# Hybrid decoder layer: fourth query projection ahead of the third x projection, and one y projection beside the last value products

## The chip, the cores and the metric

The kernel runs on one core of a Trainium2 chip. The core has five engines with instruction queues of their own: TensorE (PE; its weight loads are listed as PEld), VectorE (DVE), ScalarE (ACT), GpSimd (POOL) and SyncE (SP, which here only issues DMAs). Each queue runs in the order in which it was written. The metric is the device time of one execution in microseconds (us); the median of several runs counts.

## The reference

One layer works on 16 meta tokens and 1024 tokens of width 1024. What bears on this case:

```python
u = rmsnorm(h, g_pre_mix[l])
z = u @ w_in[l]
q, k, v, xr, yr = jnp.split(z, split_at, axis=-1)     # 512, 128, 128, 512, 512 columns
attn = sliding_window_attention_with_sinks(q, k, v, attn_sinks[l])   # window 128, 8 heads
xr = causal_depthwise_conv(xr, conv_w[l], conv_b[l])  # 4 taps
hr = rg_lru(xr, w_a[l], b_a[l], w_x[l], b_x[l], lru_lambda[l])
rec = (jax.nn.gelu(yr.astype(jnp.float32)) * hr).astype(h.dtype)
mix = jnp.concatenate([attn.astype(h.dtype), rec], axis=-1) @ w_out[l]
h = h + rmsnorm(mix, g_post_mix[l])
...
f = jnp.square(jax.nn.relu(u @ w_ff1[l])) @ w_ff2[l]
h = h + rmsnorm(f, g_post_ffn[l])
```

The recurrence `rg_lru` computes two sigmoid gates from `xr`, a decay from one of them, and a scan along the tokens.

## The kernel before

Everything is float32. For each product an operand is split into a high part (a cast on ACT, L95) and a low part (a subtraction on DVE, L98), and three matmuls (L124 to L126) stand for one.

**The input projection** is cut into chunks of 128 columns. Queries, x and y have four chunks each. A chunk is 48 matmuls of width 512 for queries and y (two pieces, `REAL2`), and 96 matmuls of width 272 or 256 for x (four pieces, `ALL`). The pieces go to the two PSUM banks of the tag "acc". Keys, values, query chunk 0 and x chunk 0 are computed first. A finished piece is evicted: a query piece by two scaled casts on ACT (L116) and two subtractions on DVE (L117), an x piece by a copy on ACT (L394), a y piece by a copy on DVE (L640). Behind each x chunk follows its convolution, four DVE passes (`conv`, L608 and L613).

**Attention** runs over four head pairs j and two halves of the tokens. `scores(j, half, q)` makes the query-key products (L525, L529), the maximum, the exponential on ACT (through `lut`, L82) and a folding of the two window blocks on POOL (L559). `attend(j, half, pairs)` transposes the result (L571), splits it, masks it on POOL (L575) and makes the value products (L585), which are evicted by L598 and L599. It is called one step late, behind the next step's scores.

**Fills.** The remaining projections are put between the steps of attention. `fills` (L648 to L655) is their list: q1, x1, q2, x2, x3, q3 and then y0 to y3. Each call of `next_fill` (L658) issues the load, cast and low part of the following entry's weights and then the matmuls, evictions and convolution of its own entry. Eight calls stand in the attention loop, under `deferred(FILL_LAG)`; the two last, y2 and y3, stand behind the gates (L753).

**What sets the order.** A planner lays out each engine's queue before the run: of the instructions whose inputs and buffers are ready in its own model of time, the one with the lowest order number goes first. The number counts up as the program is written; inside `deferred` it is 1000 higher. So a fill is used where attention has nothing ready. On the chip the order is fixed, and an engine that waits for one instruction does not go on to the next. Buffers have tags, with a fixed count for each tag, and the buffers of a tag go round in the order of the program. Those that matter here are the tag "raw" (2, weights as loaded), "ws" (4, split weights), "d" (4: results of the convolutions 0 to 2, the raw x chunk of 1 to 3, and y0, y2, y3), and "b" (17: among others keys, values, the query pairs, attention's results, convolution 3 and y1).

**Behind attention** come the gates (`gates`, four times: split of the convolved chunk, matmuls, sigmoids), the decays (`decay`), the scan (`recur`), the product with the y chunks (`rec_out`, which ends in a split into `at[half][2]` and `at[half][3]`), the output weights (`load_wo`, `split_wo`) and the output projection `out_mm`. Its first half (kc 0 to 3, `at[half][0]` and `[1]`) needs attention alone; its second half needs the recurrent result. `lut` puts all table functions of ACT into one chain in the order of the program. The feed-forward part, two thirds of the time, follows.

```python
    for j in range(NPAIR):
        for half in range(2):
            if j % 2 == 0 and half == 0:
                at_pair(j // 2)
            sn = scores(j, half, qs[j])
            if True:
                with deferred(FILL_LAG):
                    next_fill()
            if prev is not None:
                attend(*prev)
            prev = (j, half, sn)
    attend(*prev)
```

Of the kernel before, what the change touches and what calls it, by code (L numbers as in the profile page):

```python
# [29 lines left out]
FILL_LAG = 1000  # L30
# [7 lines left out]
def hybrid_layer(  # L38
# [7 lines left out]
    x, out = x[0], out[0]  # L46
# [11 lines left out]
    def slot(tag, shape, dt=F32):  # L58
        uid[0] += 1
        return slab.tile(shape, dt, tag=tag, name=f"{tag}{uid[0]}", bufs=bufs[tag])  # L60

    def pair(tag, shape):
        return slot(tag, shape, F32R), slot(tag, shape, F32R)

    def bank(tag, shape=(P, 512)):
        uid[0] += 1
        return ps.tile(list(shape), F32, tag=tag, name=f"ps_{tag}{uid[0]}")

    def f32(ap):
        return ap.bitcast(F32)  # L70

    @contextmanager
    def deferred(n):
        tc.cur_priority += n
        yield
        tc.cur_priority -= n
# [16 lines left out]
    def split(hi, lo, src, eng=None):  # L93
        if eng is None:
            nc.scalar.copy(hi, src)  # L95
        else:
            eng.tensor_copy(hi, src)
        low = nc.vector.tensor_tensor(lo, src, f32(hi), op=ALU.subtract).ins  # L98
        mark[0] = low.name
        return low  # L100
# [90 lines left out]
    def w_q(j):  # L191
        return load_cols([((w_in, Q_COL + P * j), P)])

    def w_x_chunk(c):
        return load_cols([((w_in, X_COL + P * c), P)])
# [307 lines left out]
    def at_pair(cp):  # L503
        for half in range(2):
            at[half][cp] = pair("b", [P, 2, 512])
# [58 lines left out]
    def attend(j, half, pairs):  # L564
        g = j // 2
        o_ = slot("e", [P, 512])
        for bp, sn in enumerate(pairs):
            mh, ml = pair("c", [P, 4, 2, P])
            pt = bank("pt", (P, 4, P))
            for k in range(4):  # L570
                nc.tensor.transpose(pt[:, k, :], sn[:, k, 0:P], ident)  # L571
            split(mh[:, :, 1, :], ml[:, :, 1, :], pt)
            for m in (mh, ml):
                for side, op, sign in ((0, ALU.is_gt, 1), (1, ALU.is_ge, -1)):
                    nc.gpsimd.affine_select(  # L575
                        out=m[:, :, side, :], in_=f32(m)[:, :, 1, :],
                        pattern=[[0, 4], [-sign, P]], compare_op=op, fill=0.0,
                        base=0, channel_multiplier=sign,
                    )
            po = bank("o", (P, 2, 256))  # L580
            mhv, mlv = (m.rearrange("p (h i) s q -> p h (i s q)", h=2) for m in (mh, ml))

            def av(v, oc, n, pc, first, last):
                for k, m in enumerate((mhv, mlv)):
                    nc.tensor.matmul(  # L585
                        po[:, :, oc : oc + n], v, m[:, :, pc : pc + n],
                        start=first and k == 0, stop=last and k == 1,
                        skip_group_check=True,
                    )

            b = 4 * half + 2 * bp
            av(vk[g][:, b, :], 0, 256, P, True, False)
            av(vm[:, g, :] if b == 0 else vk[g][:, b - 1, :], 0, P, 0, False, False)
            av(vk[g][:, b + 1, :], P, P, 3 * P, False, True)
            c = slice(256 * bp, 256 * bp + 256)
            for h in range(2):
                r, o = HALF[h], HALF[1 - h]
                nc.scalar.copy(o_[r, c], po[o, h, :])  # L598
                nc.vector.tensor_tensor(o_[r, c], po[r, h, :], o_[r, c], op=ALU.add)  # L599
        ah, al = at[half][j // 2]  # L600
        split(ah[:, j % 2, :], al[:, j % 2, :], o_)
# [19 lines left out]
    def fill_q(j):  # L621
        def run(w):
            q, sink = new_q()
            project(w, REAL2, sink)
            qs[j] = q
        return run

    def fill_x(c):
        def run(w):
            xr, sink = new_x()  # L630
            project(w, ALL, sink)
            conv(c, xr, "b" if c == 3 else "d")
        return run
# [12 lines left out]
    qs = [q0] + [None] * 3  # L646
    conv(0, xr0)
    fills = []  # L648
    for kind, j in (("q", 1), ("x", 1), ("q", 2), ("x", 2), ("x", 3), ("q", 3)):
        if kind == "q":  # L650
            fills.append((lambda j=j: w_q(j), fill_q(j)))
        else:
            fills.append((lambda j=j: w_x_chunk(j), fill_x(j)))
# [4 lines left out]
    def next_fill():  # L658
        i = len(loaded) - 1
        if i + 1 < len(fills):  # L660
            loaded.append(fills[i + 1][0]())
        else:
            loaded.append(None)
        fills[i][1](loaded[i])

    prev = None
# [8 lines that stand above are left out]
            if prev is not None:  # L675
                attend(*prev)
            prev = (j, half, sn)
    attend(*prev)


# [14 lines left out]
    def gates(c):  # L695
        ch, cl = pair("b", [P, TT])
        split(ch, cl, xc[c])
        rg[c] = []
        for i in range(2):
            t_ = slot("c", [P, TT])  # L700
            for t0, n in ((0, 348), (348, 348), (696, 344)):
                flip[0] += 1
                acc = bank(("s", "pt", "o")[flip[0] % 3])
                mm3(
                    acc[:, :n], (gh[:, i, c, :], gl[:, i, c, :]),
                    (ch[:, t0 : t0 + n], cl[:, t0 : t0 + n]), True, True,
                )
                lut(
                    t_[:, t0 : t0 + n], acc[:, :n], AF.Sigmoid,
                    bias=prm[:, c, 5 + i : 6 + i],  # L710
                )
            rg[c].append(t_)
        nc.vector.tensor_tensor(t_, t_, xc[c], op=ALU.mult)
# [36 lines left out]

    for c in range(NLRU):
        gates(c)
    for _ in range(2):  # L753
        next_fill()
    for cs in ((0, 1), (2, 3)):
        for c in cs:
            decay(c)
# [597 lines left out]
```

## Time and profile before

| what | before |
|---|---|
| median of 3 runs | 976.04 us (975.72 to 976.45) |
| profiled execution, its own time | 983.92 us |
| profiled execution, its span | 982.2 us |
| PE busy | 951.9 us, 97% of the span |
| DVE, ACT, POOL busy | 662.9, 500.5, 140.3 us |
| attention with its fills | about 62 to 218 us of the span |
| gates to the recurrent result | 218 to 282 us |
| output projection, first matmul | 244.7 us |

Durations are read from one profiled execution, the time of the kernel from the median of the runs. Positions are microseconds from the start of the span. A line such as `L585` is a line of the kernel; where a helper such as `split` or `mm3` writes the instruction, it is the helper's line, and the tile names tell which use it is. Buffer numbers are left out of the names, so that "d" stands for any buffer with the tag "d", and "ps_acc" for a bank with the tag "acc". An idle time in brackets is how long the engine stood still ahead of that instruction, and behind it stands what ended the wait.

### The profile page before, as it was taken

The page shows a single profiled execution, that of the slowest core. Times are in us where ns is not written, and L with a number is a line of the kernel's source. Part 1 is how long each engine was busy: PE and PEld are TensorE (multiplying, and loading weights), DVE is VectorE, ACT ScalarE, POOL GpSimd, SP SyncE. Part 2 cuts the span into 40 slices and gives each one's busy share as a digit, 9 for nine tenths or more (in the row PEclk, how much of TensorE's full clock was granted, in tenths as well). Part 3 has the DMA queues.
Part 4 walks back from the last instruction along what each step waited for, and adds up shares of the span by engine and source line. Part 5 has one row for each costly group of instructions (what it writes and reads, how often), then busy time and mean ns, then how long its engine had stood idle before and what let it go on. Part 6 is the DMA issues. An engine that isn't in the chain of part 4 may idle for free.

```text
span 982.2 us, 12324 instructions
## 1 busy us (share of the span) xinstructions
PE 951.9 (97%) x4654; PEld 797.1 (81%) x4654; DVE 662.9 (67%) x942; ACT 500.5 (51%) x816; POOL 140.3 (14%) x184
## 2 busy tenths in 40 slices
PE   6999989999899999999999999999999999999996
PEld 6998988888788887887788888888888788888885
DVE  5569976755876687656554455468567666779885
ACT  6556562548935554343455556555433343445432
POOL 4016753230002100000000000000011000003011
PEclk9999989999999999999999999999999999999999
DMA  8111001112234465575532264423678766656653
GB/s 282 49 46 42 22 23 44 33 43 65 86 107 150 150 215 192 172 243 192 187 129 86 85 200 121 129 86 108 164 180 194 166 222 207 177 168 150 168 175 85
DMA packets 84794, 131.30 MB, mean 134 GB/s; under 512 B 5464, under 2 KB 48616, under 8 KB 84736
## 3 DMA queue, kind: packets, MB, share of 16 engines
q1 hardware_dynamic: 76912, 109.55, 34.7%
q0 software_dynamic: 7248, 19.40, 9.7%
q10 hardware_dynamic: 576, 1.57, 0.4%
q8 instruction: 36, 0.59, 0.3%
q14 instruction: 22, 0.18, 0.1%
HBM read 110.46 MB, written 18.87 MB: 132 GB/s over the span
## 4 chain that ended last, share of the span: by engine, by line
PE 80%; DVE 7%; ACT 5%; DMA 3%; issue 3%; POOL 2%; DVEq 0%; SPq 0%; ACTq 0%; POOLq 0%
PE ps_acc L124 8%; PE ps_acc L125 8%; PE ps_acc L126 8%; PE ps_pt L125 6%; PE ps_pt L126 6%; PE ps_pt L124 6%; PE ps_s L126 6%; PE ps_s L125 6%; PE ps_s L124 6%; PE ps_o L125 5%; PE ps_o L124 5%; PE ps_o L126 5%; DMA d<-in_w_ff_dram 2%; ACT c L82 1%; DVE ws L98 1%
## 5 line engine op out<-in xcount | busy, mean ns | idle before, releaser
L95 ACT CAST ws<-raw 128x1024 fp32r<-128x1024 f32 (+1 forms) x70 | 71.7, 1024 | 128.1 <-PE ps_o L125 47.5
L98 DVE TENSOR_TENSOR ws<-raw,ws 128x1024 fp32r<-128x1024 f32 (+1 forms) x71 | 85.0, 1197 | 46.4 <-ACT ws L95 46.3
L124 PE MATMUL ps_acc<-a,ws 128*128 128x256 f32 (+2 forms) x256 | 87.6, 342 | 1.4 <-ACT d L394 1.3
L125 PE MATMUL ps_acc<-a,ws 128*128 128x256 f32 (+2 forms) x256 | 86.9, 339 | 0.0
L126 PE MATMUL ps_acc<-a,ws 128*128 128x256 f32 (+2 forms) x256 | 86.2, 337 | 0.0
L98 DVE TENSOR_TENSOR b<-b,b 128x1024 fp32r<-128x1024 f32 (+2 forms) x48 | 57.6, 1200 | 26.3 <-PE ps_o L125 20.1
L95 ACT CAST ws<-e 128x1024 fp32r<-128x1024 f32 x42 | 43.9, 1045 | 59.2 <-PE ps_o L125 35.0
L95 ACT CAST b<-b 128x1024 fp32r<-128x1024 f32 (+2 forms) x48 | 49.5, 1030 | 39.0 <-DVE b L861 38.1
L98 DVE TENSOR_TENSOR ws<-e,ws 128x1024 fp32r<-128x1024 f32 x42 | 51.3, 1222 | 16.1 <-ACT ws L95 16.1
L124 PEld LDWEIGHTS ps_acc<-a,ws 128*128 128x128 f32 x256 | 50.1, 196 | 6.1 <-ACT d L394 1.7
L169 POOL TENSOR_TENSOR rs<-ms,half_pow 128x1 f32<-128x1 f32 (+1 forms) x31 | 22.8, 739 | 221.3 <-DVE ms L165 219.9
L575 POOL TENSOR_SCALAR_AFFINE_SELECT c<-c 128x512 fp32r<-128x512 f32 x64 | 49.7, 794 | 27.9 <-ACT c L95 12.5
L126 PEld LDWEIGHTS ps_acc<-a,ws 128*128 128x128 f32 x256 | 49.9, 195 | 4.5
L125 PEld LDWEIGHTS ps_acc<-a,ws 128*128 128x128 f32 x256 | 50.1, 196 | 4.0
L1122 POOL DMA_DIRECT2D raw<-in_w_ff_dram x9 | 11.0, 1218 | 265.5 <-DVE ws L98 206.0
L125 PE MATMUL ps_acc<-ws,b 128*128 128x512 f32 (+1 forms) x120 | 46.2, 385 | 1.2 <-DVE ws L98 1.2
L126 PE MATMUL ps_acc<-ws,b 128*128 128x512 f32 (+1 forms) x120 | 46.3, 386 | 0.0
L124 PE MATMUL ps_acc<-ws,b 128*128 128x512 f32 (+1 forms) x120 | 46.2, 385 | 0.0
L125 PE MATMUL ps_pt<-ws,b 128*128 128x512 f32 x112 | 44.1, 394 | 0.0
L126 PE MATMUL ps_pt<-ws,b 128*128 128x512 f32 x112 | 44.1, 393 | 0.0
L124 PE MATMUL ps_pt<-ws,b 128*128 128x512 f32 x112 | 44.0, 393 | 0.0
L124 PE MATMUL ps_s<-ws,b 128*128 128x512 f32 x110 | 43.4, 395 | 0.0
(388 smaller groups left out, 2740.0 us busy)
## 6 DMA issues: line engine op xcount, KB each, us to landing
raw<-in_w_ff_dram SPq DMA_DIRECT2D x66, 512.0 KB, 4.2
e<-in_w_ff_dram SPq DMA_DIRECT2D x47, 512.0 KB, 3.7
raw<-in_w_in_dram SPq DMA_DIRECT2D x12, 512.0 KB, 4.6
d<-in_w_ff_dram SPq DMA_DIRECT2D x12, 512.0 KB, 4.8
s_dram<-d POOLq DMA_DIRECT2D x12, 512.0 KB, 4.1
raw<-in_w_ff_dram POOLq DMA_DIRECT2D x9, 512.0 KB, 6.6
c<-in_x_dram SPq DMA_DIRECT2D x8, 512.0 KB, 8.1
d<-in_x_dram SPq DMA_DIRECT2D x8, 512.0 KB, 3.5
```

The lines of the kernel that those rows point to most:

```text
L82: ins = nc.scalar.activation(*args, **kwargs).ins
L95: nc.scalar.copy(hi, src)
L98: low = nc.vector.tensor_tensor(lo, src, f32(hi), op=ALU.subtract).ins
L124: nc.tensor.matmul(dst, lh, rh, start=start, stop=False, skip_group_check=True)
L125: nc.tensor.matmul(dst, lh, rl, start=False, stop=False, skip_group_check=True)
L126: last_mm[0] = nc.tensor.matmul(dst, ll, rh, start=False, stop=stop, skip_group_check=True).ins.name
L169: last_pow[0] = nc.gpsimd.tensor_tensor(rs[:n], ms[:n], half_pow[:n], op=ALU.pow).ins.name
L575: nc.gpsimd.affine_select(out=m[:, :, side, :], in_=f32(m)[:, :, 1, :], pattern=[[0, 4], [-sign, P]], compare_op=op, fill=0.0, base=0, cha ...
L1122: nc.gpsimd.dma_start(raws[0], w2v[q, a, b], accum_op=ADD)
```

## The change

The list of fills is put in another order: q3 stands ahead of x3. In the loop, the step j = 2, half 0 now calls the fill q3, and j = 2, half 1 calls x3. Since each fill issues its follower's weights, the load, cast and low part of q3's weights are now issued with x2, those of x3 with q3, and those of y0 with x3.

The fill y2 is called behind the loop, ahead of the last `attend`, and there it is under `deferred(FILL_LAG)`. With it the weights of y3 are issued there, under the same number. Behind the gates one call is left, y3.

```diff
     fills = []
-    for kind, j in (("q", 1), ("x", 1), ("q", 2), ("x", 2), ("x", 3), ("q", 3)):
+    for kind, j in (("q", 1), ("x", 1), ("q", 2), ("x", 2), ("q", 3), ("x", 3)):
         if kind == "q":
             fills.append((lambda j=j: w_q(j), fill_q(j)))
         else:
@@ -675,6 +675,8 @@
             if prev is not None:
                 attend(*prev)
             prev = (j, half, sn)
+    with deferred(FILL_LAG):
+        next_fill()
     attend(*prev)
 
 
@@ -750,8 +752,7 @@
 
     for c in range(NLRU):
         gates(c)
-    for _ in range(2):
-        next_fill()
+    next_fill()
     for cs in ((0, 1), (2, 3)):
         for c in cs:
             decay(c)
```

## The prediction

> **What bounds the kernel now.** I read the page's first part, then TensorE's (PE's) waits in order of time, then a table of stages, and last what ScalarE (ACT) and VectorE (DVE) did where PE stood still.
>
> ```profile
> span 982.2 us, 12324 instructions
> PE 951.9 (97%) x4654; PEld 797.1 (81%) x4654; DVE 662.9 (67%) x942; ACT 500.5 (51%) x816; POOL 140.3 (14%) x184
> ```
>
> PE works 97% of the span, and the change adds and removes no matmul. It can therefore only take away or add time in which PE stands still or runs at a lower clock. These are PE's stops around the edit, in the timeline (start, duration, instruction, in brackets the idle time before it and what ended it):
>
> ```profile
> 91.52 0.36 PE L525 MATMUL ps_s<-b,b 128*128 128x256 f32 x1 [0.43 <-DVE rden L555]
> 92.65 0.39 PE L124 MATMUL ps_acc<-a,ws 128*128 128x256 f32 x1 [0.42 <-ACT d L394]
> 130.02 0.35 PE L525 MATMUL ps_s<-b,b 128*128 128x256 f32 x1 [1.57 <-ACT b L116]
> 131.59 0.58 PE L124 MATMUL ps_acc<-a,ws 128*128 128x256 f32 x1 [0.85 <-ACT d L394]
> 155.59 0.47 PE L585 MATMUL ps_o<-c,b 128*128 128x512 f32 x1 [0.67 <-POOL c L575]
> 157.70 1.27 PE L585 MATMUL ps_o<-c,b 128*128 128x512 f32 x5 [1.65 <-POOL c L575]
> 220.44 0.43 PE L124 MATMUL ps_s<-b,e 128*128 128x348 f32 x1 [0.22 <-ACT b L95]
> 222.49 0.43 PE L125 MATMUL ps_s<-b,e 128*128 128x348 f32 x1 [0.83 <-DVE b L98]
> 269.80 0.50 PE L124 MATMUL ps_pt<-a,b 128*128 128x512 f32 x1 [2.65 <-ACT b L95]
> ```
>
> The last five are behind the place of the edit. Call them A (155.59 and 157.70, value products waiting for POOL's masks), B (220.44 and 222.49, the gates) and C (269.80, the output projection waiting for the recurrent half). The next view cuts the time at the edges where the granted clock (third figure from the end, before DMA) changes. Its columns are the stretch, its length, then busy time and count of PE, weight loads, DVE, ACT and POOL.
>
> ```profile
> 89.91:93.33 3.42, 2.58 (x18) 2.16 (x18) 3.32 (x11) 2.45 (x8) 2.72 (x4) 1.00 0.52 153
> 127.46:130.88 3.42, 1.70 (x12) 1.30 (x11) 3.36 (x11) 3.21 (x12) 1.27 (x1) 1.00 0.37 107
> 130.88:134.29 3.41, 2.70 (x12) 2.70 (x13) 3.29 (x11) 2.85 (x10) 1.28 (x1) 0.50 0.18 51
> 134.29:137.70 3.41, 3.41 (x18) 3.41 (x17) 1.08 (x3) 0.45 (x2) 0.00 (x0) 0.50 0.00 0
> 154.77:158.18 3.41, 1.09 (x6) 0.62 (x5) 2.73 (x4) 0.75 (x2) 2.81 (x3) 1.00 0.00 0
> 158.18:161.60 3.42, 3.42 (x19) 3.42 (x18) 1.19 (x3) 1.37 (x4) 0.00 (x0) 0.50 0.00 0
> 267.41:270.82 3.41, 1.02 (x4) 0.86 (x5) 3.05 (x4) 3.40 (x6) 0.00 (x0) 1.00 0.00 0
> 270.82:274.24 3.42, 3.42 (x9) 2.67 (x8) 3.42 (x4) 0.40 (x1) 0.00 (x0) 0.50 0.51 153
> ```
>
> Where PE worked only 1.70, 1.09 or 1.02 us of such a stretch, the next ran at half clock; after 2.58 us it did not, nor behind B. A half-clock stretch of 3.42 us loses 1.71 us of work. So A costs 0.67 + 1.65 + 1.71 = 4.03 us, B 0.22 + 0.83 = 1.05 us, C 2.65 + 1.71 = 4.36 us: together 9.44 us.
>
> The Trainium skill (TensorE: Matmul & The Clock Gate, "HAM oscillation — how this bites in real kernels") gives as a rule that PE-idle gaps beyond about 3.4 us bring the clock down. The trace differs: gaps of 1.65 and 2.65 us stand ahead of half-clock stretches. What the rule would make of the sum is weighed among the rivals.
>
> **Part 1: the fourth query projection ahead of the third x projection.** Why stop A exists shows in ACT and DVE:
>
> ```profile
> 157.24 0.39 ACT L394 COPY d<-ps_acc 128x272 f32<-128x272 f32 x1 [1.92 <-DVE d L613]
> 155.47 1.68 DVE L613 SCALAR_TENSOR_TENSOR d<-d,prm,d 128x1037 f32<-128x1037 f32 x1
> ```
>
> x projection 3 follows x projection 2 at 146.16 at once. Its first piece is to be copied into a "d" buffer (four of them), which comes free only when convolution 2 has ended at 157.15 (155.47 + 1.68). Until then both "acc" banks are full, the third piece can't start, and PE has nothing to lay between the value products. After the change q projection 3 stands there. It writes "b" buffers: one is free, the other comes free with the second q pair, whose scores are through by then. So its matmuls can fill A. How many, and where the rest moves, comes from the stages (same columns; the block below them counts the instructions on "acc" banks alone):
>
> ```profile
> 146.16:158.77 12.61, 10.29 (x76) 9.59 (x75) 10.95 (x15) 4.62 (x10) 9.75 (x10) 0.98 0.14 42
> 158.77:165.70 6.93, 6.93 (x49) 6.93 (x49) 1.19 (x3) 1.75 (x5) 0.00 (x0) 0.80 0.00 0
> 165.70:176.75 11.05, 11.05 (x51) 9.03 (x50) 8.54 (x9) 3.68 (x7) 0.00 (x0) 1.00 0.18 49
> 176.75:217.60 40.85, 40.76 (x211) 34.27 (x210) 24.98 (x62) 19.05 (x51) 16.03 (x21) 1.00 0.14 38
> 217.60:244.73 27.13, 26.07 (x132) 22.34 (x131) 15.73 (x16) 23.47 (x36) 0.00 (x0) 1.00 0.22 71
> 244.73:267.15 22.42, 22.42 (x97) 17.87 (x95) 20.16 (x19) 22.30 (x26) 0.00 (x0) 1.00 0.29 94
> ```
>
> ```profile
> 146.16:158.77 12.61, 6.82 (x50) 6.36 (x49) 0.00 (x0) 0.76 (x2) 0.98 0.14 42
> 220.22:244.73 24.51, 11.24 (x49) 8.96 (x48) 1.97 (x3) 0.00 (x0) 1.00 0.21 65
> ```
>
> q projection 3 is the third row: 11.05 us. Attention's own matmuls beside it are 10.29 - 6.82 = 3.47 us. It then ends at 146.16 + 11.05 + 3.47 = 160.7 instead of 176.75, and the last head pair's scores, which followed its end at once, start 16 us earlier. POOL stood at 0.00 from 158.77 to 176.75, and DVE and ACT were loosely used; that hole closes. A: -4.03 us.
>
> C hangs on ACT's chain from the gates to the split of the recurrent result, which starts when the last value product has been evicted:
>
> ```profile
> 218.38 1.05 ACT L95 CAST e<-e 128x1024 fp32r<-128x1024 f32 x1 [0.80 <-DVE b L98]
> 269.13 0.61 ACT L95 CAST b<-d 128x512 fp32r<-128x512 f32 x1
> ```
>
> Moved by 16 us, the second cast is at 253.1. PE needs it when its own work is done: from 146.16 the stages hold 10.29 + 6.93 + 11.05 + 40.76 - 1.71 (the half clock) + 26.07 + 22.42 = 115.8 us, so at 262.0 without a stop. That leaves 8.9 us for the chain to slip. C: -4.36 us. In B, PE had run out of projections. The first four of those terms, 67.3 us, now end at 213.5, 11 us behind the gates' first cast at 202.4, so there is filler: -1.05 us.
>
> What the order adds: an x projection behind a q projection whose evictions (two ACT and two DVE instructions a piece) hold the banks while the first x piece is short. This transition has two rows: at 91.52 it cost 0.43 + 0.42 = 0.85 us at full clock; at 130.02 it cost 1.57 + 0.85 = 2.42 us and two half-clock stretches, 3.41 us, together 5.83 us. Same instructions, same loaded DVE (3.32 and 3.36 of 3.42 us busy); nothing in the rows says which the new place is nearer to, so I take the middle, 3.34 us, and keep 0.85 and 5.83 for the range.
>
> x projection 3 now stands ahead of y projection 0, which also needs a "d" buffer, freed by convolution 3. Convolution 2 ended 11.0 us after its projection. y projection 0 offers 11.05 us of matmuls before the banks block, and attention adds 6.9 us in 40.85 (40.76 less 33.87 of "acc", row below), some 1.9 us in 11: cover 12.9 us against 11.0. I cost it at nothing; without that cover it is a second A, 4.03 us.
>
> ```profile
> 176.75:217.60 40.85, 33.87 (x135) 24.32 (x135) 4.14 (x6) 1.19 (x2) 1.00 0.14 38
> 213.43 1.05 ACT L95 CAST ws<-raw 128x1024 fp32r<-128x1024 f32 x1 [3.20 <-PE ps_acc L125]
> 242.96 1.03 ACT L95 CAST a<-raw 128x1024 fp32r<-128x1024 f32 x1
> 243.90 1.16 ACT L82 ACTIVATE c<-c,m4sp 128x1040 f32<-128x1040 f32 x1
> 261.21 1.28 ACT L82 ACT_TABLE_LOAD   x1
> raw<-in_w_in_dram SPq DMA_DIRECT2D x12, 512.0 KB, 4.6
> ```
>
> The weight load that each projection issues for its follower swaps with it: SP's queue holds the same 512 KB transfers in another order, a stage or more ahead of their casts; POOL's queue has none of them. Nothing.
>
> **Part 2: a y projection ahead of the last value products.** Before, y projection 2 already ran as filler there, though written behind the gates: "acc" matmuls are 33.87 us of the stage up to 217.60, three times 11.05. So the move of its matmuls is worth nothing. But it also issues the load, cast and low part of y projection 3's weights, and these now carry 1000 more in the order number, behind the gates, the decays and the output weights. Before, that cast ran at 213.43. Raw and weight buffers go round in program order, so the output weights wait behind it. I cost it at nothing: at 242.96 a cast of output weights, written behind the decays, was let in ahead of one of them, and ACT was idle for 27.13 - 23.47 = 3.7 us of that stage.
>
> **Sum.** -4.03 - 1.05 - 4.36 + 3.34 = -6.10 us. The profiled execution took 983.92 us, 982.2 of it span; the median is 976.04, 0.8% less. PE's stops lie in both, so I take the difference off the median unscaled: 969.9 us.
>
> **The rivals.** *The hole only moves* (22%). Convolution 3 shares DVE with the last pair's attention, y projection 0 blocks as x projection 3 did, and the q-to-x transition costs its upper row: 976.04 - 1.05 - 4.36 + 5.83 = 976.5. For it: DVE is the busier engine in the new stage. Against it: twice the filler. PE's later stops, behind 330, are four groups of waits (total, times, longest), of which the first and the last are:
>
> ```profile
> PE ps_acc L125 <- DVE ws L98: 1.2, 1, 1.2
> ...
> PE ps_acc L124 <- ACT a L1044: 0.7, 1, 0.7
> ```
>
> The four add up to 3.7 us; since later work is ordered anew too, they can vanish or double.
>
> *The last y weights come too late* (18%), the slower one. If ACT takes the delayed cast only behind the whole chain of activations (the table load at 261.21, now 16 us earlier, 245.2), y projection 3 starts after the cast and an equal DVE pass, 247.3. PE has run out of other work at 262.0 - 22.42 - 11.24 + 3.34 = 231.7. It stops for 15.6 us and a half-clock stretch: 969.9 + 15.6 + 1.7 = 987.2. It decides from a cast later than 229.6, 27 us into the chain. Against it: the row at 242.96.
>
> *The half-clock stretches stay* (5%). If they have another cause than the stops, only stops count: -(2.32 + 1.05 + 2.65) plus the middle of 0.85 and 2.42, 1.64: -4.4, so 971.7. By the skill's rule above, no gap here is long enough, and this would be the outcome; the trace, with three stops followed by three drops, speaks against it.
>
> **How the numbers follow.** The forecast holds 55%; its own range is 967.5 (0.85 for the transition) to 972.4 (5.83). 0.2% is 2 us, about what a measurement of this kernel can tell from no change. Faster by more: 55 + 5 = 60%. Of the moved hole's 22%, 14 lie within 0.2% and 8 above, where later stops double. With the late weights slower has 26%. The range leaves out the late weights: from 967.5 less most of the later stops, 964.5, to 976.5 plus most of them, 979.5.
>
> **What would show it.** Right: "acc" matmuls of width 512 between the value products near 155 with no wait for POOL; the last pair's first scores near 161; the gates' first cast near 202; no wait of PE for ACT's casts ahead of the output projection's second half; half clock fewer than three times. Wrong: PE waiting for ACT or DVE near 160 with two half-clock stretches; a copy into "d" waiting for the third convolution; or the cast of the last y weights, after 229, with PE idle ahead of it.

## The result, and the profile after

The changed kernel takes 967.05 us (median of six executions, 964.76 to 969.23). Before, measured beside it, takes 976.25 us (975.48 to 981.53). The ratio is 0.990, with a 95% interval of 0.988 to 0.992: 9.2 us faster. The profiled execution of after took 966.77 us.

First the page of after, its span and its first part, and then PE's timeline from x projection 1 to the output projection (start, duration, instruction, in brackets the idle time ahead of it and what ended it). The plain rows stand for the first and the last matmuls of q projection 3, value products between them, the first scores of the last head pair and the first matmul of x projection 3; the rows with brackets are the stops from 89 us on that were there before too, and two new ones at the end.

```profile
span 965.0 us, 12324 instructions
PE 943.2 (98%) x4654; PEld 791.5 (82%) x4654; DVE 663.6 (69%) x942; ACT 501.1 (52%) x816; POOL 144.4 (15%) x184
```

```profile
89.19 0.36 PE L525 MATMUL ps_s<-b,b 128*128 128x256 f32 x1 [0.43 <-DVE rden L555]
90.33 0.39 PE L124 MATMUL ps_acc<-a,ws 128*128 128x256 f32 x1 [0.42 <-ACT d L394]
127.69 0.35 PE L525 MATMUL ps_s<-b,b 128*128 128x256 f32 x1 [1.57 <-ACT b L116]
129.26 0.58 PE L124 MATMUL ps_acc<-a,ws 128*128 128x256 f32 x1 [0.86 <-ACT d L394]
142.62 0.39 PE L124 MATMUL ps_acc<-a,ws 128*128 128x512 f32 x1
...
153.01 0.39 PE L124 MATMUL ps_acc<-a,ws 128*128 128x512 f32 x1
153.24 0.86 PE L585 MATMUL ps_o<-c,b 128*128 128x512 f32 x5
153.94 0.39 PE L125 MATMUL ps_acc<-a,ws 128*128 128x512 f32 x1
...
156.26 0.39 PE L126 MATMUL ps_acc<-a,ws 128*128 128x512 f32 x1
156.49 0.22 PE L525 MATMUL ps_s<-km,b 128*128 128x128 f32 x1
...
158.81 0.29 PE L124 MATMUL ps_acc<-a,ws 128*128 128x272 f32 x1
...
236.72 0.50 PE L125 MATMUL ps_pt<-ws,b 128*128 128x512 f32 x1 [0.56 <-DVE ws L98]
...
248.66 0.72 PE L124 MATMUL ps_pt<-a,b 128*128 128x512 f32 x2 [0.59 <-ACT a L95]
```

The value products (`L585`) no longer wait for POOL: the 512-wide matmuls of q projection 3 stand between them. The stops A, B and C are gone. In their place there are two stops of 0.56 and 0.59 us in the output projection, for the low part and the cast of weights. The table of stages shows how dense that part is now (length, then busy time and count of PE, weight loads, DVE, ACT and POOL, granted clock): q projection 3 with the value products beside it, and behind it a stretch in x projection 3, the new place of the transition.

```profile
142.62:156.49 13.87, 13.87 (x71) 11.55 (x69) 12.24 (x18) 5.82 (x13) 9.93 (x10) 1.00 0.14 40
158.81:162.22 3.41, 3.41 (x30) 3.41 (x29) 3.28 (x9) 2.57 (x9) 0.26 (x1) 1.00 0.42 122
```

PE is busy for all of both. What comes behind is on VectorE's and ScalarE's timelines: the last step of convolution 3 and the first eviction of y projection 0, and then the first cast of the gates and the cast of the last y weights.

```profile
184.37 1.35 DVE L613 SCALAR_TENSOR_TENSOR b<-d,prm,b 128x1037 f32<-128x1037 f32 x1
...
186.94 0.69 DVE L640 COPY d<-ps_acc 128x512 f32<-128x512 f32 x1
```

```profile
195.86 1.05 ACT L95 CAST e<-e 128x1024 fp32r<-128x1024 f32 x1 [0.80 <-DVE b L98]
...
200.77 1.05 ACT L95 CAST ws<-raw 128x1024 fp32r<-128x1024 f32 x1 [0.98 <-PE ps_acc L125]
```

The two profiled executions are 17.2 us apart (983.92 and 966.77), the medians 9.2. Part of the larger figure is chance. At 89.19, ahead of the edit, after is already 2.33 us earlier than before at 91.52. The half clock differs between executions too; the last experiments show how.

### The profile page after: what moved, and what is told of

It reads as the page before. It is cut to its first block, busy times and chain, and to the rows that moved or that the text cites. A ratio compares the mean times of both kernels' runs of the same rounds, so it can differ in the third digit from the quotient of the medians.

```text
span 965.0 us, 12324 instructions
## 1 busy us (share of the span) xinstructions
PE 943.2 (98%) x4654; PEld 791.5 (82%) x4654; DVE 663.6 (69%) x942; ACT 501.1 (52%) x816; POOL 144.4 (15%) x184
## 3 DMA queue, kind: packets, MB, share of 16 engines
q10 hardware_dynamic: 576, 1.57, 0.4%
## 4 chain that ended last, share of the span: by engine, by line
PE 87%; DVE 6%; ACT 4%; DMA 1%; issue 1%; POOL 0%; DVEq 0%; SPq 0%; ACTq 0%
PE ps_acc L124 10%; PE ps_acc L125 10%; PE ps_acc L126 10%; PE ps_s L126 6%; PE ps_s L125 6%; PE ps_pt L124 6%; PE ps_pt L126 6%; PE ps_s L124 6%; PE ps_pt L125 6%; PE ps_o L126 5%; PE ps_o L124 5%; PE ps_o L125 5%; ACT c L82 1%; DVE c L545 1%; DMA b<-t_dram 1%
## 5 line engine op out<-in xcount | busy, mean ns | idle before, releaser
L95 ACT CAST ws<-raw 128x1024 fp32r<-128x1024 f32 (+1 forms) x70 | 71.8, 1026 | 117.7 <-PE ps_o L125 42.9
L124 PE MATMUL ps_acc<-a,ws 128*128 128x256 f32 (+2 forms) x256 | 86.4, 337 | 1.3 <-ACT d L394 1.3
L125 PE MATMUL ps_acc<-a,ws 128*128 128x256 f32 (+2 forms) x256 | 86.0, 336 | 0.0
L126 PE MATMUL ps_acc<-a,ws 128*128 128x256 f32 (+2 forms) x256 | 85.4, 334 | 0.0
L95 ACT CAST ws<-e 128x1024 fp32r<-128x1024 f32 x42 | 43.9, 1045 | 60.0 <-PE ps_o L125 31.5
L95 ACT CAST b<-b 128x1024 fp32r<-128x1024 f32 (+2 forms) x48 | 49.5, 1031 | 37.9 <-DVE b L862 37.2
L575 POOL TENSOR_SCALAR_AFFINE_SELECT c<-c 128x512 fp32r<-128x512 f32 x64 | 54.0, 862 | 25.3 <-DVE c L98 9.6
L124 PEld LDWEIGHTS ps_acc<-a,ws 128*128 128x128 f32 x256 | 49.1, 192 | 6.0 <-ACT d L394 1.7
L126 PEld LDWEIGHTS ps_acc<-a,ws 128*128 128x128 f32 x256 | 49.0, 191 | 4.5
L125 PEld LDWEIGHTS ps_acc<-a,ws 128*128 128x128 f32 x256 | 49.0, 191 | 3.9
```

The lines of the kernel that those rows point to most:

```text
L124: nc.tensor.matmul(dst, lh, rh, start=start, stop=False, skip_group_check=True)
L125: nc.tensor.matmul(dst, lh, rl, start=False, stop=False, skip_group_check=True)
L126: last_mm[0] = nc.tensor.matmul(dst, ll, rh, start=False, stop=stop, skip_group_check=True).ins.name
L575: nc.gpsimd.affine_select(out=m[:, :, side, :], in_=f32(m)[:, :, 1, :], pattern=[[0, 4], [-sign, P]], compare_op=op, fill=0.0, base=0, cha ...
```

## The experiments

**e1, part 1 alone.** On before, only the order of the fills is changed.

```diff
-    for kind, j in (("q", 1), ("x", 1), ("q", 2), ("x", 2), ("x", 3), ("q", 3)):
+    for kind, j in (("q", 1), ("x", 1), ("q", 2), ("x", 2), ("q", 3), ("x", 3)):
```

> Part 1 alone: q3 ahead of x3, y2 stays behind the gates. Theory (part 1 carries the whole gain, because it gives the value products of the third pair a filler and starts the last pair earlier): 967 to 968, within 1 us of the changed kernel's 967.05, with the stops A (near 155), B (near 220) and C (near 270) gone. Rival (the gates need y2 as filler, so part 2 is worth stop B and part of C): 969 to 972, with a stop of PE at the gates or ahead of the output projection's second half.

Measured: 966.51 us (963.61 to 968.35), ratio 0.988 (0.986 to 0.991). That is the whole gain of the change. In the waits of PE the three stops are gone; the output projection waits once for ACT, for 0.3 us (columns: engine, tile and line, what it waited for, total, times, longest).

```profile
PE ps_pt L124 <- ACT b L95: 0.3, 1, 0.3
```

**e2, part 2 alone.** On before, y projection 2 is called ahead of the last `attend`, in the old order of fills.

```diff
+    with deferred(FILL_LAG):
+        next_fill()
     attend(*prev)
...
-    for _ in range(2):
-        next_fill()
+    next_fill()
```

> Part 2 alone: the order of fills as before, y2 called under the delayed number ahead of the last value products. Theory (y2 ran there already, so the move is worth nothing): 976.2, within 1 us of before, with stops A and C as in the profile before. Rival 1 (it is worth stop B): 975.2. Rival 2 (the last y weights, now behind the gates in number, come late): 978 or more, with a stop of PE ahead of y3.

Measured: 976.82 us (971.04 to 981.41), ratio 0.999 (0.997 to 1.001): nothing. A, B and C are all there, as PE's waits show; A's two stops are in the row of POOL, B in that of DVE b, C in that of ACT b `L95`.

```profile
PE ps_pt L124 <- ACT b L95: 2.6, 1, 2.6
PE ps_o L585 <- POOL c L575: 2.2, 2, 1.6
...
PE ps_s L125 <- DVE b L98: 0.9, 1, 0.9
```

So y projection 2 was a filler already, and the delayed weights of y projection 3 cost nothing.

**e3, the buffer of A.** On before, convolution 2 and not convolution 3 writes into a "b" buffer. x projection 3 then finds its "d" buffer free, in the old order.

```diff
-            conv(c, xr, "b" if c == 3 else "d")
+            conv(c, xr, "b" if c == 2 else "d")
```

> The kernel before, with the order of fills untouched; only convolution 2 writes a buffer of the tag b and convolution 3 one of the tag d, the other way round than before. x projection 3 then need not wait for convolution 2 to give back its buffer. Theory (stop A exists because the third x projection was blocked by that buffer, and not because POOL is slow): stop A, 2.32 us and its half-clock stretch of 1.71, goes, B and C stay: 972.2 to 973.9. Rival (the masks on POOL are late whatever lies between): 976.2, and PE still waits some 2.3 us for POOL near 155.

Measured: 973.93 us (971.77 to 976.98), ratio 0.996 (0.995 to 0.998), just above the range expected; how little A's half clock was worth stands in the next section. PE's timeline at the last value products of that half:

```profile
153.95 0.39 PE L585 MATMUL ps_o<-c,b 128*128 128x512 f32 x1
154.18 0.28 PE L126 MATMUL ps_acc<-a,ws 128*128 128x256 f32 x1
154.30 0.28 PE L124 MATMUL ps_acc<-a,ws 128*128 128x256 f32 x1
154.44 0.96 PE L585 MATMUL ps_o<-c,b 128*128 128x512 f32 x5
```

A is gone without a word changed in the order: x projection 3's own 256-wide pieces fill the holes. So A came from the blocked "d" buffer; POOL's masks take their time in either kernel, and are hidden when there is filler. B and C stay (C below). What is left of the gain, B and C, comes only with the new order, in which the last head pair starts earlier.

```profile
262.39 0.61 PE L124 MATMUL ps_pt<-a,b 128*128 128x512 f32 x1 [2.64 <-ACT b L95]
```

**e4, work laid into C.** On before, twelve matmuls with a block of zeros, added to a bank of the output projection, stand where C is. The result is the same numbers plus zero; PE has work in the place of the stop.

```diff
         out_mm(t, pos[t], range(4))
+    for _ in range(12):
+        nc.tensor.matmul(
+            pos[3][1][0:64], km[:, 0, 0, 0:64], wo[0][0][:, 512:1024],
+            start=False, stop=False, skip_group_check=True,
+        )
```

> The kernel before, with 12 matmuls of a zero block of 64 columns added behind the first half of the output projection, where stop C is; they add zeros to a bank and take 12 x 0.23 = 2.8 us, as long as the stop. Theory (a half-clock stretch follows from PE standing still in the stretch ahead of it): PE's wait of 2.65 us shrinks or goes, no half-clock stretch near 270, time 1.7 us below before: 974.5. Rival (the half clock has another cause, as by the Trainium skill's rule no gap here is long enough): the clock still drops near 270, and the time is 976.2 or above.

Measured: 976.14 us (973.41 to 979.7), ratio 0.999 (0.997 to 1.002). The zero products fill C, but they do not shorten it: they are the first row below, and the projection's next matmul starts at 264.89, 2.83 us after they began. Behind them stand two new short stops of 0.20 and 0.40 us (the second is the second row). So the run can only save half clock, and the profiled execution has none there.

```profile
262.06 2.94 PE L962 MATMUL ps_s<-ws,km 128*64 128x512 f32 x12
...
273.65 0.51 PE L124 MATMUL ps_pt<-a,b 128*128 128x512 f32 x1 [0.40 <-ACT b L95]
```

But this execution has no half clock behind A either, where nothing was changed: two stretches of 3.413 us, the first with A's first stop and half of its second, the next with the rest of it, are

```profile
150.07:153.48 3.41, 2.00 (x12) 1.42 (x11) 3.35 (x3) 0.37 (x1) 3.34 (x4) 1.00 0.00 0
153.48:156.89 3.41, 2.60 (x21) 2.56 (x22) 1.49 (x5) 1.76 (x5) 0.75 (x1) 1.00 0.00 0
```

both at full clock. So a stop of 1.65 us does not always bring a half-clock stretch, and taking the stop away need not give 1.7 us. By itself this profile settles nothing more; it led to the next two. The granted clocks of the ten timed executions say more, and are in the next section.

**e6 and e7, before and after profiled once more**, unchanged.

> The kernel before, unchanged, profiled once more. Theory (half clock follows a grid of 3.413 us windows whose phase differs from execution to execution; a window with TensorE at half of its time or less is followed by one at half clock): the stops A, B and C are again near 2.3, 1.0 and 2.65 us, but the windows of half clock behind the transition near 130, behind A and behind C need not all be there: where the stop lies across two windows with over 0.54 of work in each, none follows. Rival (the half clock hangs on the length of the stop alone): the same three places with half clock, four windows in all.

> The kernel after, unchanged, profiled once more. Theory of the grid: the stops near 89 and 127 are there again (0.85 and 2.4 us), A, B and C are not, and half clock stands at most behind the stops near 127, for none, one or two windows. The stops behind 330 us come to less than 1 us if the new order has removed them, and anywhere from 0 to 4 us if they differ from execution to execution. Rival: one window of half clock near 130, as in the first profile.

Measured: before 973.51 us, after 967.16 us, one execution each. The pages' first lines, before and then after:

```profile
span 971.8 us, 12324 instructions
PE 944.5 (97%) x4654; PEld 789.9 (81%) x4654; DVE 663.4 (68%) x942; ACT 500.0 (51%) x816; POOL 140.9 (14%) x184
```

```profile
span 965.5 us, 12324 instructions
PE 942.8 (98%) x4654; PEld 790.2 (82%) x4654; DVE 663.9 (69%) x942; ACT 500.7 (52%) x816; POOL 145.4 (15%) x184
```

In the second profile of before, A, B and C are the same to 0.02 us (both stops of A, the longer one of B, and C):

```profile
150.78 0.47 PE L585 MATMUL ps_o<-c,b 128*128 128x512 f32 x1 [0.66 <-POOL c L575]
152.89 0.50 PE L585 MATMUL ps_o<-c,b 128*128 128x512 f32 x1 [1.64 <-POOL c L575]
...
216.14 0.43 PE L125 MATMUL ps_s<-b,e 128*128 128x348 f32 x1 [0.83 <-DVE b L98]
...
263.46 0.50 PE L124 MATMUL ps_pt<-a,b 128*128 128x512 f32 x1 [2.65 <-ACT b L95]
```

Yet only one stretch of half clock stands behind them, where the first profile had four. The stages of the second profile, cut in steps of 3.413 us counted back from the drop of the clock at 264.86: the transition and the stretch behind it, A's second stop and the stretch behind it, C and the stretch behind it.

```profile
124.91:128.32 3.41, 1.83 (x15) 1.64 (x14) 3.30 (x9) 3.21 (x11) 1.26 (x1) 1.00 0.20 58
128.32:131.74 3.42, 2.56 (x22) 2.36 (x21) 3.29 (x10) 2.84 (x10) 1.23 (x1) 1.00 0.34 101
148.80:152.22 3.42, 1.79 (x11) 1.26 (x9) 3.36 (x3) 0.37 (x1) 3.35 (x4) 1.00 0.00 0
152.22:155.63 3.41, 2.74 (x22) 2.69 (x23) 1.51 (x5) 1.76 (x5) 0.62 (x1) 1.00 0.00 0
261.44:264.86 3.42, 1.40 (x6) 1.19 (x7) 3.06 (x4) 3.41 (x6) 0.00 (x0) 1.00 0.00 0
264.86:268.27 3.41, 3.41 (x10) 2.65 (x9) 3.41 (x3) 0.02 (x1) 0.00 (x0) 0.50 0.44 154
```

The stop at the transition and A lie across two windows here, each with 1.79 us of work or more, and none is followed by half clock. C falls into one window and leaves 1.40 us: half clock follows. The rival of e6, that the length of the stop decides, falls. The later stops of the first profile, 2.9 of those 3.7 us, are not there in this one: they were no property of before. The second of after has 0.68 us there, as the first had, and one more stop of 0.34. In the second profile of after the half clock stands once, near 130, as in the first. That is what the rival said of e7, and the theory, which allowed none to two, says nothing against it: e7 does not decide between them.

**e5, a wider first piece.** On after, each x projection among the fills is cut into 512, 272 and 256 columns and not into 272 and three times 256.

```diff
+    FILL3 = [(0, 512), (512, 272), (784, 256)]
...
-            project(w, ALL, sink)
+            project(w, FILL3, sink)
```

> The kernel after, with each x projection among the fillers cut into pieces of 512, 272 and 256 columns and not 272, 256, 256 and 256. Theory (the stops of TensorE at the start of an x projection come from its short first piece, which is laid before the banks of the projection ahead of it are evicted): in the kernel after these stops are 0.43 + 0.42 us near 89 and 1.57 + 0.86 us near 127; with twice the matmuls in the first piece the sum of 3.3 us falls to 1.6 us or less, and the time to 967.05 - 1.7 = 965.4 us or less. Rival (ScalarE and VectorE are simply late there, whatever the size of the piece): the 3.3 us stay or grow, since one wide piece takes a whole bank for longer, and the time is 967 us or above.

Measured: 964.08 us (962.78 to 964.95), ratio 0.987 (0.986 to 0.989), 3 us under after, whose one execution in the same series (e7) took 967.16. PE's waits and, below, its first stop in the timeline:

```profile
PE ps_o L586 <- POOL c L576: 1.1, 2, 0.9
PE ps_pt L124 <- ACT b L95: 0.8, 1, 0.8
```

```profile
116.82 0.50 PE L586 MATMUL ps_o<-c,b 128*128 128x512 f32 x1 [0.88 <-POOL c L576]
```

The stops at both transitions, 0.85 and 2.43 us in after, are gone; the old cut was their cause. The new one has a wider first piece and one piece fewer, with its eviction; no run parts the two. In their place stands a wait for POOL of 1.1 us in two parts, and the output projection waits 0.8 us for ACT, where after has 0.56 + 0.59. That is 2.5 us less in all, most of the 3 us. No half clock stands in its profile but at the ends.

**e8, part 1 with the wider piece**, the edits of e1 and e5 together, without part 2.

> Before, with the fourth query projection ahead of the third x projection (part 1 alone) and the wider first piece of the x projections. Theory: part 2 is worth nothing, so this gives the same time as the wider piece on the kernel after, within 0.2%: 965 us. Rival (the short stops of 0.5 us that part 2's place left in the output projection matter): 0.5 to 1 us less than on the kernel after.

Measured: 963.82 us (962.74 to 964.59), ratio 0.987 (0.985 to 0.989). It is the fastest by its median, but 0.26 us from e5 is within what these runs can tell: part 2 is worth nothing here too. Both beat after.

## Why the prediction was right, and where it was not

The time, 967.05 us, is in the range, on the side forecast, and 2.9 us under the number. It is also 0.4 us under 967.5, where the forecast's own terms end, since these still charge the transition with 0.85 us. The gain was forecast at 6.1 us and is 9.2. Point by point:

- **A, B and C as stops** (2.32 + 1.05 + 2.65 = 6.02 us): right. All three are gone in after and in e1. The reason given for A, the "d" buffer, is confirmed by e3, where freeing it removes A alone; that B and C go because the last pair is earlier is what e1 and e3 leave, but no run moves the last pair alone.
- **The new place of q projection 3**: right. It takes 13.87 us, where 11.05 + 3.47 = 14.5 was worked out; 512-wide matmuls fill the place of A.
- **The transition from q to x, +3.34 us**: this step failed. It cost nothing, less than the lower end of 0.85. Finding VectorE loaded alike at both old places and nothing to tell them apart, the prediction took the middle of their costs. VectorE is as loaded at the new place (3.28 of 3.41 us busy behind 158.81), and PE still never stopped. ScalarE's room alone does not explain it: it is busy for 2.57 us there, and for 2.45 in the prediction's row of 89.91, where PE did stop. What differs from the old place near 127 is the rows above: 2.3 us of attention stand between the last matmul of q projection 3 (156.26) and the first of x projection 3 (158.81), while at the old place the x projection follows at once (the two rows below this list). The prediction had named the short first piece as one of two conditions, and e5 shows that the cut into pieces decides at the old places. Why the same cut does no harm at the new one, this attention or something else, no run here tests. The upper cost of 5.83 us was also 0.36 too high: in the window of 130.88 PE was busy for 2.70 us, so half clock took 1.35 us of work there and not 1.71.
- **The half clock, 1.71 us each for A and for C**: the mechanism was right and the size was not. It was read from one execution, in which the windows had fallen badly (four stretches). e6 has the same stops with one stretch, e4 the transition and A with none. The rule that the prediction took, one drop for each long stop, is too strict. By the table below, A's half clock was worth some 0.4 us on average and C's some 2.4, each uncertain by about half a microsecond; behind C no profile shows more than one stretch, 1.71 us.
- **y projection 0 behind convolution 3, nothing**: right. The convolution ends at 185.72, y projection 0 is evicted from 186.94, and PE does not stop.
- **Part 2, nothing**: right (e2). The late cast, at 200.77, follows the gates' first casts, ahead of the table load, and no y projection waits for it. The slower rival, which had it behind the whole chain, falls.
- **The rivals of the faster side**: the hole did not move, there was filler enough. That the half clock stays whatever the stops do (by the Trainium skill's rule that the prediction cites, gaps this short should bring none) falls too: it comes with the stops, only not with each, and e4, which fills C with work as long as C was, loses less to half clock.
- **Later stops can vanish or double**: true, but not through the change, as e6 shows. The two small new stops, 0.56 + 0.59 = 1.15 us, were in no term of the sum.

```profile
120.39 0.39 PE L126 MATMUL ps_acc<-a,ws 128*128 128x512 f32 x1
120.62 0.29 PE L124 MATMUL ps_acc<-a,ws 128*128 128x272 f32 x1
```

Then where do 9.2 us come from? e6 and e7 have one stretch of half clock each, and are 973.51 - 967.16 = 6.35 us apart. By the pages, 971.8 - 944.5 = 27.3 us and 965.5 - 942.8 = 22.7 us are idle, so 4.6 us of it are stops: 6.02 less the new 1.15, within 0.3. The other 1.7 us are busy time of the same matmuls, some of which run longer where they stand next to stops. The groups of PE's instructions from 120 to 300 us show 0.3 us of it for the value products, in before's second profile and in after's; the rest is not followed up here:

```profile
L585 PE MATMUL ps_o<-c,b 128*128 128x512 f32 x18 | 7.2, 411 | 2.4 <-POOL c L575 2.3
```

```profile
L585 PE MATMUL ps_o<-c,b 128*128 128x512 f32 x18 | 6.9, 402 | 0.1
```

The rest, 9.2 - 6.35 = 2.9 us, is half clock, as far as the granted clocks tell. The record has the mean granted clock of every timed execution. One less this clock, times the span, estimates the work lost to half clock (the clock is given to 0.001, about 1 us, and the half clock at the end of every execution is in it). The averages:

| kernel | executions | time, us | lost to half clock, us |
|---|---|---|---|
| before (beside e1 to e8) | 38 | 976.8 | 6.8 |
| e3, without A | 12 | 973.9 | 6.4 |
| e4, C filled with work | 10 | 976.1 | 4.4 |
| after (with e7) | 7 | 966.8 | 3.9 |

After loses 2.9 us less than before, uncertain by about half a microsecond, as are the other differences. That this equals the rest so closely is luck, as the average times lie 10.0 us apart and the medians 9.2. Among before's executions the time follows the clock: three at 0.996 took 974.1 us on average, sixteen at 0.994 took 975.7, four at 0.990 took 980.6. It fits the profiles: before has three places where a stretch of half clock can start, after has one; four stretches were seen in one profile of before and one in the other, one in each of after, none in e1. In e4 the rest of the time is 1.7 us longer than in before, which hides most of what it saved; its two new stops are 0.6 of that, the remainder is not followed up.

So one term carries the miss of 3.1 us: 3.34 us too much was charged for the transition. The other errors nearly cancel, and that is luck. The half clock was charged at 3.42 us and is worth some 2.9, less of it for A than charged and more for C. The new stops, 1.15 us, and what the stops' neighbours lose, 1.7 us, were in no term, and work against each other.

## What to carry to other kernels

When a bounding engine waits for a slow helper, ask first what filler was due there and which buffer kept it out: here the wait named POOL, and a buffer's tag elsewhere removed it. Look at where a piece of filler starts: a wider first piece, two lines of code, was worth 3 us more. And before a stop is charged with a clock penalty from one profile, profile the same kernel again, or read the granted clock of every timed execution: the stops A, B and C repeat to 0.02 us, the penalty does not.

## What was not expected of the hardware

The granted clock changes only at the edges of a grid of 3.413 us. In the profile of before the three drops at 130.88, 158.18 and 270.82 are 8.00 and 33.00 such steps apart (41 steps are 139.94 us). The grid does not start with the kernel: A's second stop ends 0.67 us behind an edge in e6 (152.89 and 152.22), and 2.93 us behind one in the first profile of before (157.70 and 154.77).

The Trainium skill (TensorE: Matmul & The Clock Gate, "What's actually happening") describes such a free-running window of 3413 ns that does not reset when a kernel starts. The runs here agree: the step is 3.413 us, and its edges fall elsewhere in the two executions of before.

What decides is PE's work within one window, by the busy time that the profile gives. The nearest cases from both sides are the row of e6 at 148.80 above (1.79 us, full clock follows), this row of e1 (1.85 us, full clock follows) and, below it, two rows of e2:

```profile
124.17:127.58 3.41, 1.85 (x15) 1.66 (x14) 3.21 (x9) 3.22 (x11) 1.28 (x1) 1.00 0.16 44
```

```profile
127.20:130.61 3.41, 1.75 (x13) 1.35 (x11) 3.35 (x11) 3.20 (x12) 1.27 (x1) 1.00 0.34 99
130.61:134.02 3.41, 2.66 (x12) 2.66 (x13) 3.28 (x11) 2.85 (x10) 1.29 (x1) 0.50 0.21 60
```

With 1.75 us of 3.41 the next window is at half clock, with 1.79 it is not: in these runs the border lies between 0.51 and 0.52 of a window. Counted over the ten profiled executions, without their heads and tails, 11 windows at full clock held 0.23 to 0.51 of work, and half clock followed each; 30 held 0.52 to 0.78, and it followed none. From half clock the way back asks for more: the second row of e2, 2.66 us busy at half clock, is followed by another window of half clock (the prediction's row of 130.88, with 2.70, too), while at full clock 2.56 us in e6 kept it. A window of half clock that is busy throughout, as the one at 264.86 in e6, is followed by full clock, and so is the one of e7 with 3.02 us.

So the same two stops at the transition, 1.57 and 0.85 us, are followed by no half-clock window in e6, by one in after and by two in the first profile of before, by where they fall. With the clocks above, that goes far to explain why before scatters over some 9 us between executions (973.19 to 982.88 in the 29 that stand beside the first four experiments) and e5, without such a stop, over 2.
